# Six raw weight tiles instead of four and four split gated tiles instead of two, in a streaming-encoder layer on one Trainium2 core

## The chip, the core and the metric

The kernel runs on one core of a Trainium2 chip. A core has five engines that each work through their own list of instructions in order: TensorE (PE in the profile, with PEld for its weight loads) multiplies matrices, VectorE (DVE) and ScalarE (ACT) work on elements, GpSimd (POOL) does a little of it here, and SyncE (SP) issues nearly all the transfers, which sixteen DMA engines carry out. The metric is the device time of one execution in microseconds: the median of the runs, smaller is better.

## What is computed

One layer of a hybrid encoder on 256 tokens of width 4096, in float32. An input projection feeds 16 heads of forgetting attention (fox), 32 heads of an RWKV-7 recurrence, and a gate z; the gated outputs go through an output projection and a residual LayerNorm.

```python
proj = jnp.einsum('bsd,dc->bsc', x, w_in)
fox_cols, rw_cols, z = proj[..., :fox_end], proj[..., fox_end:fox_end + SHIFT_COLS], proj[..., fox_end + SHIFT_COLS:]
...
fox_out = _fox_attention(fq, fk, fv, log_f)
...
rw = rw + (rw_prev - rw) * mu_shift
...
y = _rwkv7_scan(rh, decay, kh, vh, -kk, kk * ah)
...
h = jnp.concatenate([fox_out, rwkv_out], axis=-1) * jax.nn.silu(z)
out = jnp.einsum('bsc,cd->bsd', h, w_out)
x = _layernorm(ALPHA * x + out, ln_gain, ln_bias, LN_EPS)
```

## The kernel before

**Precision.** Both projections are made of three matmuls for each product. A float32 tile is split into a high part (a cast to fp32r on ACT, suffix h) and a low part (the difference, on DVE, suffix l), and PE sums x_high times w_high, x_low times w_high, and x_high times w_low.

**Stages.** The first block, with the low-rank columns, runs from w_first. Then the loop at L1284 goes over eight groups n (two RWKV head pairs and two fox heads each), with four blocks b of 512 columns: b 0 holds r and k, b 1 the two kinds of v, b 2 and 3 fq, fk and the two halves of z for one fox head each. Behind the groups, the output projection (L1318) takes eight blocks of 512 columns, wo. In the trace a weight tile is w_q or wo_q, with q from 0 to 15: a tile is 128 rows by 1024 columns, two steps of 128 of the contraction, 512 KB, and feeds 12 matmuls of 512 columns.

**The weight stream.** load (L608) issues a weight's transfer into a raw tile of the tag wr, four buffers. fetch (L615) keeps up to three raw tiles waiting and splits the oldest (split, L521: four high buffers, three low ones). weights (L632) keeps three split tiles ready and hands the next to the matmuls. A raw buffer is free again once both its cast and its difference are done, and the next transfer into it waits for that on SyncE.

**Side work.** Between the matmuls of the blocks, slot (L592) advances generators: prepare turns r and k into the recurrence's operands, rwkv runs the recurrence of one group, fox the attention of one head, unload turns the projected columns by way of memory. In prepare the tile raw (r and k, turned) is loaded, ACT and DVE make the token shift s from it, then DVE forms k, sb and shl, and PE sums shl over head channels into np. In unload a fox head's fq is loaded (L1207), ACT scales it (L1211), and PE forms the scores fsp from it.

**The gate.** gate (L767) multiplies an output of either kind by its gate into h and splits h into hl. For a channel tile k below FAR (29), hl is stored to memory (hd, L780) and loaded back (h, get_h, L1217) while the last block runs, into the room of the x tiles that it no longer needs; the others stay on chip. The tag hl has two buffers, and the generator goes on only while fewer than two stores are under way.

**What sets the order.** All calls are only recorded (Later.take, L232). flush (L275) then makes an order for each engine from estimated durations, keeping a list of free buffers for each tag, and issues the instructions in it (L371), so every one of them has L372 in the profile. PE's main matmuls stand in their given order and side matmuls are placed between them. More buffers of a tag thus change the order that the planner writes as well as the waits on the chip.

**Room.** The program reserves, unless told otherwise, 16 KiB of each partition of the on-chip memory as a scratch for dynamic transfers that GpSimd issues. This kernel issues none from there: it issues its transfers from SyncE and, at the very start, two from ScalarE.

Of the kernel before, what the change touches and what calls it, by code (L numbers as in the profile page):

```python
# [12 lines left out]
F32 = mybir.dt.float32  # L13
# [6 lines left out]
P = 128  # L20
# [446 lines left out]
def layer(ctx: ExitStack, tc: tile.TileContext, xt, xtok, w_first, w_main, muv, w_o, up, par, mulora, fbias, lng, lnb, cst, out):  # L467
    nc = Later(tc)
# [4 lines left out]
    xpool = ctx.enter_context(tc.tile_pool(name="xpool", bufs=1))  # L473
    wpool = ctx.enter_context(tc.tile_pool(name="wpool", bufs=3))
# [19 lines left out]
    for n, (k0, k1) in enumerate(pieces):  # L494
        raw = spool.tile([P, 2 * S], F32, tag="xr", name=f"xr{n}", bufs=4)
        nc.sync.dma_start(out=raw[:, : (k1 - k0) * S], in_=xt[:, k0:k1, :].rearrange("p k t -> p (k t)"))
        x_raw.append(raw)
        raw = spool.tile([P, 4 * HALFB], F32, tag="fr", name=f"fr{n}", bufs=4)
# [22 lines left out]
    def split(src, n, name, pool=wpool, tag="", cols=1024):  # L521
        hi = pool.tile([P, cols], F32R, tag="wh" + tag, name=name + "h", bufs=4 if pool is wpool else 1)
        lo = pool.tile([P, cols], F32R, tag="wl" + tag, name=name + "l")
        nc.scalar.copy(hi[:, :n], src[:, :n])
        nc.vector.tensor_tensor(lo[:, :n], src[:, :n], hi[:, :n].bitcast(F32), ALU.subtract)
        return hi, lo
# [58 lines left out]
    def wait(n):  # L585
        for _ in range(n):
            yield
# [11 lines left out]
    stream = [(f"w{n}_{b}_{q}", w_main[n, b][:, 2 * q : 2 * q + 2, :]) for n in range(G // 2) for b in range(4) for q in range(KT // 2) if n or b]  # L599
# [6 lines left out]
    raws = []  # L606

    def load():  # L608
        if stream:
            name, src = stream.pop()  # L610
            raw = wpool.tile([P, 1024], F32, tag="wr", name=name, bufs=4)
            nc.sync.dma_start(out=raw, in_=src.rearrange("p k c -> p (k c)"))
            raws.append((name, raw))

    def fetch():  # L615
        while len(raws) < 3 and stream:
            load()
        if raws:
            name, raw = raws.pop(0)
            if name not in kept:  # L620
                ready.append((name, *split(raw, 1024, name)))
                return
            hl = []
            for j in range(4):
                hl.append(xpool.tile([P, OB], F32R, tag=f"x{4 * kept[name] + j}", name=f"{name}_{j}"))
            for j in range(2):
                r = raw[:, j * OB : (j + 1) * OB]
                nc.scalar.copy(hl[j], r)
                nc.vector.tensor_tensor(hl[2 + j], r, hl[j].bitcast(F32), ALU.subtract)
            ready.append((name, hl[:2], hl[2:]))  # L630

    def weights(name):  # L632
        nc.sooner = AHEAD
        while len(ready) < 3 and (stream or raws):
            fetch()
        nc.sooner = 0
        got, hi, lo = ready.pop(0)
        assert got == name
        return hi, lo
# [17 lines left out]
    rp = mid.enter_context(tc.tile_pool(name="rp", bufs=1))  # L657
# [18 lines left out]
    def issue(out, src):  # L676
        nc.sync.dma_start(out=out, in_=src)
# [77 lines left out]
    storing = []  # L755
# [10 lines left out]

    def gate(y, key, k):  # L767
        far = k < FAR
        while len(storing) > 1:
            yield  # L770
        h = rp.tile([P, S], F32, tag="h", name=f"h{k}")
        nc.vector.scalar_tensor_tensor(h, y, 0.5, szs[key], ALU.mult, ALU.mult)
        pool, tag, bufs = (rp, "hl", 2) if far else (xpool, f"x{k}", 1)
        hl = pool.tile([P, 2, S], F32R, tag=tag, name=f"hl{k}", bufs=bufs)
        nc.scalar.copy(hl[:, 0, :], h)
        nc.vector.tensor_tensor(hl[:, 1, :], h, hl[:, 0, :].bitcast(F32), ALU.subtract)
        if far:
            storing.append(k)
            yield from wait(SENT)
            issue(hd[k], flat(hl).bitcast(F32))  # L780
            kept_h.add(k)
            storing.remove(k)
        else:
            ht[k] = hl
# [6 lines left out]
    def flat(t):  # L791
        return t.rearrange("p a b -> p (a b)")
# [108 lines left out]
    def rwkv(n):  # L901
# [199 lines left out]
        for u in range(2):  # L1101
            nc.vector.reciprocal(sd[:, u], sd[:, u])
            yield
            nc.vector.tensor_tensor(yc[:, u], yc[:, u], sd[:, u], ALU.mult)
            nc.vector.tensor_tensor(yc[:, u], yc[:, u], bon[:, u], ALU.add)
            while f"r{i0 + u}" not in szs or 2 * (i0 + u) + 1 >= FAR and not closed:
                yield
            yield from gate(yc[:, u], f"r{i0 + u}", 2 * (i0 + u) + 1)
# [4 lines left out]
    def fox(i, q, k, vt):  # L1113
# [32 lines left out]
        while f"f{i}" not in szs or 2 * i >= FAR and not closed:  # L1146
            yield
        yield from gate(o, f"f{i}", 2 * i)
        foxed.add(i)

# [167 lines left out]
    for b, q in outs:  # L1318
        if q == 0:
            pool, tag = (ps, "ps") if b == 1 or b and b % 2 == 0 else (pp, "pp")  # L1320
# [3 lines left out]
        for j in range(2):  # L1324
            k = 2 * q + j
# [106 lines left out]
    for t, (i, h) in enumerate(order):  # L1432
# [10 lines left out]
        k, j, hi, lo = late[i]  # L1443
# [77 lines left out]
```

## Time and profile before

| | before |
|---|---|
| median of 3 runs, us | 1923.37 |
| lowest and highest, us | 1923.21, 1923.68 |
| the profiled execution, us | 1923.9 |
| its span from first to last instruction, us | 1922.1 |
| mean granted TensorE clock | 1.000 |
| share of the chain that ended last: PE | 95% |
| the same: DMA | 2% |
| read from and written to HBM, MB | 397.48, 38.26 |

The profile's page gives each engine's busy time. The windows view gives the same for chosen stretches. The waits view says which instruction waited for what and for how long. The chain view follows the work that ended last back in time, and the timeline shows single instructions with the idle time of their engine before them and what ended it in brackets. A row is read as start, duration, engine, line, operation, and what it writes and reads, with the tiles' shapes. An engine that idles costs nothing unless PE waits for it in the end.

### The profile page before, as it was taken

To read this page: it belongs to the slowest core of one execution; us is meant where nothing else is said; L and a number is where in the kernel's file an instruction comes from. 1 tells how busy PE (TensorE), PEld (TensorE's weight loads), DVE (VectorE), ACT (ScalarE), POOL (GpSimd) and SP (SyncE) were. 2 spreads that over 40 slices of the span, in tenths; PEclk is the share of its full clock that TensorE was granted. 3 is DMA by queue.
4 is the path that set the end of the run, shared out by engine and by line. 5 is a ranking of instruction groups with operands and counts; after the bars stand their busy time and mean duration, and the time that the engine had idled before them with its cause. 6 is when DMAs were issued, how large, how long until landed. Compare 5 with 4: busy or idle time off the path is not lost.

```text
span 1922.1 us, 28038 instructions
## 1 busy us (share of the span) xinstructions
PE 1909.9 (99%) x9965; PEld 1596.5 (83%) x9965; DVE 1408.4 (73%) x2290; ACT 970.1 (50%) x1434; POOL 42.4 (2%) x88
## 2 busy tenths in 40 slices
PE   9999999999999999999999999999999999999998
PEld 9888888888888888888888888888888788888887
DVE  6597778866886788669867885698678866755555
ACT  6464465455544554455446444554464444444332
POOL 0000000000000000000000000000000000000000
PEclk9999999999999999999999999999999999999999
DMA  9678877976698779867977797679777996866664
GB/s 353 186 219 252 232 199 207 266 220 199 206 272 230 198 204 262 220 199 210 274 223 207 201 265 216 199 214 269 220 213 197 357 277 195 294 201 202 189 195 164
DMA packets 340991, 437.60 MB, mean 228 GB/s; under 512 B 211682, under 2 KB 241988, under 8 KB 340852
## 3 DMA queue, kind: packets, MB, share of 16 engines
q1 hardware_dynamic: 340564, 435.45, 77.4%
q8 instruction: 78, 1.28, 0.3%
q14 instruction: 61, 0.50, 0.1%
q10 hardware_dynamic: 288, 0.37, 0.1%
HBM read 397.48 MB, written 38.26 MB: 227 GB/s over the span
## 4 chain that ended last, share of the span: by engine, by line
PE 95%; DMA 2%; DVE 2%; ACT 0%; issue 0%; ACTq 0%; SPq 0%; POOL 0%; DVEq 0%; POOLq 0%
PE acc L372 69%; PE oacc L372 17%; PE accl L372 2%; PE yp L372 1%; PE gp L372 1%; DMA w<-in_w_main_dram 1%; PE rh L372 1%; DMA wo<-in_w_o_dram 1%; PE up L372 1%; DMA hd<-hl 1%; PE lp L372 1%; PE fsp L372 1%; PE sp L372 1%; PE fop L372 0%; PE np L372 0%
## 5 line engine op out<-in xcount | busy, mean ns | idle before, releaser
L372 PE MATMUL acc<-w_9h,x 128*128 128x512 f32 x248 | 79.1, 398 | 0.0
L372 DVE TENSOR_TENSOR prod<-Nb,xc 128x8 f32<-128x8 f32 (+30 forms) x248 | 71.9, 290 | 9.7 <-DMA Nb<-nd 4.9
L372 PE MATMUL acc<-w_15h,x 128*128 128x512 f32 x248 | 78.8, 396 | 0.0
L372 PE MATMUL acc<-w_13h,x 128*128 128x512 f32 x248 | 78.8, 394 | 0.0
L372 PE MATMUL acc<-w_11h,x 128*128 128x512 f32 x248 | 78.6, 394 | 0.0
L372 PE MATMUL acc<-w_1h,x 128*128 128x512 f32 x248 | 78.3, 392 | 0.0
L372 PE MATMUL acc<-w_8h,x 128*128 128x512 f32 x248 | 78.0, 392 | 0.0
L372 PE MATMUL acc<-w_4h,x 128*128 128x512 f32 x248 | 78.0, 392 | 0.0
L372 PE MATMUL acc<-w_5h,x 128*128 128x512 f32 x248 | 77.7, 393 | 0.0
L372 PE MATMUL acc<-w_7h,x 128*128 128x512 f32 x248 | 77.7, 392 | 0.0
L372 PE MATMUL acc<-w_10h,x 128*128 128x512 f32 x248 | 77.6, 392 | 0.0
L372 PE MATMUL acc<-w_0h,x 128*128 128x512 f32 x248 | 77.5, 392 | 0.0
L372 PE MATMUL acc<-w_12h,x 128*128 128x512 f32 x248 | 77.1, 391 | 0.0
L372 PE MATMUL acc<-w_14h,x 128*128 128x512 f32 x248 | 77.0, 391 | 0.0
L372 PE MATMUL acc<-w_3h,x 128*128 128x512 f32 x248 | 76.9, 391 | 0.0
L372 PE MATMUL acc<-w_2h,x 128*128 128x512 f32 x248 | 76.8, 389 | 0.0
L372 PE MATMUL acc<-w_6h,x 128*128 128x512 f32 x248 | 76.4, 389 | 0.0
L372 DVE TENSOR_REDUCE xc<-prod 128x8 f32<-128x16 f32 (+30 forms) x248 | 72.3, 292 | 5.1
L372 ACT CAST w_11h<-w 128x1024 fp32r<-128x1024 f32 x31 | 32.7, 1054 | 56.1 <-PE acc L372 32.9
L372 ACT CAST w_15h<-w 128x1024 fp32r<-128x1024 f32 x31 | 32.6, 1052 | 51.2 <-PE acc L372 35.7
L372 DVE TENSOR_TENSOR w_0l<-w,w_0h 128x1024 fp32r<-128x1024 f32 x31 | 37.9, 1223 | 26.0 <-PE acc L372 23.4
L372 PEld LDWEIGHTS acc<-w_6h,x 128*128 128x128 f32 x248 | 46.6, 188 | 9.7
(625 smaller groups left out, 5477.8 us busy)
## 6 DMA issues: line engine op xcount, KB each, us to landing
w<-in_w_main_dram SPq DMA_DIRECT2D x496, 512.0 KB
wo<-in_w_o_dram SPq DMA_DIRECT2D x128, 512.0 KB
bt<-bk SPq DMA_DIRECT2D x96, 128.0 KB
fr<-in_w_first_dram SPq DMA_DIRECT2D x14, 720.0 KB
Nb<-nd SPq DMA_DIRECT2D x16, 512.0 KB
hd<-hl SPq DMA_DIRECT2D x29, 256.0 KB
h<-hd SPq DMA_DIRECT2D x29, 256.0 KB
raw<-bt SPq DMA_DIRECT2D x16, 256.0 KB
```

Of the source, the lines that this page charges most:

```text
L372: ins = op.call(*op.args, **op.kwargs)
```

## The change

The tag wr has six buffers instead of four, and fetch keeps up to five raw tiles waiting instead of three. The tag hl has four buffers instead of two, and a gate waits only while more than three stores are under way. Two raw tiles of 4 KiB and two hl tiles of 2 KiB in each partition, 12 KiB together, come out of the scratch, which shrinks from 16 KiB to 1 KiB.

```diff
--- before.py
+++ after.py
@@ -608,12 +608,12 @@
     def load():
         if stream:
             name, src = stream.pop()
-            raw = wpool.tile([P, 1024], F32, tag="wr", name=name, bufs=4)
+            raw = wpool.tile([P, 1024], F32, tag="wr", name=name, bufs=6)
             nc.sync.dma_start(out=raw, in_=src.rearrange("p k c -> p (k c)"))
             raws.append((name, raw))
 
     def fetch():
-        while len(raws) < 3 and stream:
+        while len(raws) < 5 and stream:
             load()
         if raws:
             name, raw = raws.pop(0)
@@ -766,11 +766,11 @@
 
     def gate(y, key, k):
         far = k < FAR
-        while len(storing) > 1:
+        while len(storing) > 3:
             yield
         h = rp.tile([P, S], F32, tag="h", name=f"h{k}")
         nc.vector.scalar_tensor_tensor(h, y, 0.5, szs[key], ALU.mult, ALU.mult)
-        pool, tag, bufs = (rp, "hl", 2) if far else (xpool, f"x{k}", 1)
+        pool, tag, bufs = (rp, "hl", 4) if far else (xpool, f"x{k}", 1)
         hl = pool.tile([P, 2, S], F32R, tag=tag, name=f"hl{k}", bufs=bufs)
         nc.scalar.copy(hl[:, 0, :], h)
         nc.vector.tensor_tensor(hl[:, 1, :], h, hl[:, 0, :].bitcast(F32), ALU.subtract)
@@ -1508,7 +1508,7 @@
     import concourse.bacc as _bacc
     from concourse.bass_utils import run_bass_kernel_spmd as _run
 
-    nc = _bacc.Bacc("TRN2", target_bir_lowering=False, num_devices=1)
+    nc = _bacc.Bacc("TRN2", target_bir_lowering=False, num_devices=1, dynamic_dma_scratch_size=1024)
     arrays, args = {}, []
     for name, a in arrange(inputs).items():
         arrays[f"in_{name}_dram"] = a
```

The same instructions are issued, and PE's list differs at three places only, in groups 3, 5 and 7, block 1. The lists of ACT and DVE differ in some dozens of rows by a place or two, and SyncE's by two weight tiles throughout. Three places follow. In all of them the numbers behind the last underscore only number the tiles.

**Group 3, block 1, ACT.** Here hl is the split of a gated output, s_6 the shifted r and k of channel tile 6. Before:

```order
L372 CAST hl_1773<-h_1772 128x256
L372 CAST w_1_10h<-w_1_10_1833 128x1024
L372 CAST w_1_11h<-w_1_11_1839 128x1024
L372 CAST hl_1820<-h_1819 128x256
L372 ACTIVATE s_6_1824<-raw_1813,omm 128x256
L372 ACTIVATE s_6_1825<-raw_1813,omm 128x256
L372 CAST w_1_12h<-w_1_12_1842 128x1024
```

With the change:

```order
L372 CAST hl_1775<-h_1774 128x256
L372 CAST w_1_10h<-w_1_10_1816 128x1024
L372 CAST hl_1822<-h_1821 128x256
L372 CAST w_1_11h<-w_1_11_1823 128x1024
L372 ACTIVATE s_6_1826<-raw_1815,omm 128x256
L372 ACTIVATE s_6_1827<-raw_1815,omm 128x256
L372 CAST w_1_12h<-w_1_12_1835 128x1024
```

The group's third hl cast (the second one shown) now stands ahead of the cast of weight tile 11, one place earlier.

**The same block, PE.** np is the sum of shl over head channels. Before:

```order
L372 MATMUL acc_1_0_1791<-w_1_11h,x_170 128x512 x2
L372 MATMUL acc_1_0_1791<-w_1_11l,x_170 128x512
L372 MATMUL acc_1_1_1792<-w_1_11h,x_170 128x512 x2
L372 MATMUL np_1848<-shl_1836,onesr 128x512 x2
L372 MATMUL acc_1_1_1792<-w_1_11l,x_170 128x512
```

With the change:

```order
L372 MATMUL acc_1_0_1793<-w_1_11h,x_170 128x512 x2
L372 MATMUL acc_1_0_1793<-w_1_11l,x_170 128x512
L372 MATMUL np_1850<-shl_1838,onesr 128x512 x2
L372 MATMUL acc_1_1_1794<-w_1_11h,x_170 128x512 x2
L372 MATMUL acc_1_1_1794<-w_1_11l,x_170 128x512
```

The pair of np moved ahead by two matmuls. In group 5 it moves by the same two, in group 7 by three.

**Group 7, block 3, SyncE.** w_3_q are the weights of block 3, h the gated tiles that come back, fq, fk and zf the turned columns of the fox head. Before:

```order
L372 DMA w_3_11_3302<-in_w_main_dram 128x1024
L372 DMA h_3328<-hd 128x512
L372 DMA w_3_12_3307<-in_w_main_dram 128x1024
L372 DMA h_3332<-hd 128x512
L372 DMA h_3333<-hd 128x512
L372 DMA fq_3282<-bt_2_3277 128x256
L372 DMA fk_3283<-bt_2_3277 128x256
L372 DMA zf_3284<-bt_2_3277 128x256
L372 DMA w_3_13_3315<-in_w_main_dram 128x1024
```

With the change:

```order
L372 DMA w_3_13_3304<-in_w_main_dram 128x1024
L372 DMA h_3330<-hd 128x512
L372 DMA w_3_14_3309<-in_w_main_dram 128x1024
L372 DMA h_3334<-hd 128x512
L372 DMA h_3335<-hd 128x512
L372 DMA fq_3284<-bt_2_3279 128x256
L372 DMA fk_3285<-bt_2_3279 128x256
L372 DMA zf_3286<-bt_2_3279 128x256
L372 DMA w_3_15_3317<-in_w_main_dram 128x1024
```

The three small loads stand behind the same h loads, but behind weight 14, and weight 15 follows them where weight 13 did.

**Output projection, third block, SyncE.** res, lg and lbias are loads for the residual and the LayerNorm. Before:

```order
L372 DMA wo_1_3503<-in_w_o_dram 128x1024
L372 DMA wo_2_15425<-in_w_o_dram 128x1024
L372 DMA res_15410<-in_xtok_dram 128x512
L372 DMA lg_15417<-in_lng_dram 128x512
L372 DMA res_15409<-in_xtok_dram 128x512
L372 DMA res_15410<-in_xtok_dram 128x512
L372 DMA lg_15444<-in_lng_dram 128x512
L372 DMA res_15409<-in_xtok_dram 128x512
L372 DMA res_15410<-in_xtok_dram 128x512
L372 DMA res_15409<-in_xtok_dram 128x512
L372 DMA wo_3_15428<-in_w_o_dram 128x1024
```

With the change:

```order
L372 DMA wo_3_3505<-in_w_o_dram 128x1024
L372 DMA wo_4_15429<-in_w_o_dram 128x1024
L372 DMA res_15414<-in_xtok_dram 128x512
L372 DMA lg_15421<-in_lng_dram 128x512
L372 DMA res_15413<-in_xtok_dram 128x512
L372 DMA res_15414<-in_xtok_dram 128x512
L372 DMA lg_15448<-in_lng_dram 128x512
L372 DMA res_15413<-in_xtok_dram 128x512
L372 DMA res_15414<-in_xtok_dram 128x512
L372 DMA res_15413<-in_xtok_dram 128x512
L372 DMA wo_5_15432<-in_w_o_dram 128x1024
```

The loads for the residual are the same; the weights ahead of, between and behind them are each two tiles further on.

## The prediction

> **What bounds the kernel now.** I read the page first: TensorE (PE) is busy for nearly the whole span.
>
> ```profile
> span 1922.1 us, 28038 instructions
> PE 1909.9 (99%) x9965; PEld 1596.5 (83%) x9965; DVE 1408.4 (73%) x2290; ACT 970.1 (50%) x1434; POOL 42.4 (2%) x88
> ```
>
> So the change can only pay where PE stands still: 1922.1 - 1909.9 = 12.2 us in all. The table of windows of 20 us says where. Its columns are the window, its length, PE busy with the number of matmuls, the granted clock, the DMA engines' share and GB/s.
>
> ```profile
> 660.00:680.00 20.00, 18.93 (x87) 1.00 0.75 237
> 1040.00:1060.00 20.00, 19.82 (x91) 1.00 0.79 251
> 1420.00:1440.00 20.00, 19.73 (x89) 1.00 0.80 258
> 1460.00:1480.00 20.00, 20.00 (x112) 1.00 0.66 182
> 1520.00:1540.00 20.00, 18.59 (x84) 1.00 1.04 408
> 1640.00:1660.00 20.00, 19.47 (x85) 1.00 0.99 357
> 1900.00:1920.00 20.00, 14.33 (x96) 1.00 0.48 197
> ```
>
> Between the first 20 us and 1900 only five windows fall short of 20.00, all shown (1460 to 1480 stands for the full ones), by 1.07, 0.18, 0.27, 1.41 and 0.53 us: 3.46 us. The rest of the 12.2 us is the start and the tail (the last row), which the change does not reach. The waits of PE name the five:
>
> ```profile
> PE np L372 <- DVE shl L372: 1.5, 3, 1.1
> PE fsp L372 <- ACT fq L372: 1.4, 1, 1.4
> PE oacc L372 <- DVE wo_5l L372: 0.5, 1, 0.5
> ```
>
> A stall is longer than its shortfall, because a matmul's record outlasts the time until the next one may start. The chain has 54 matmuls in 12.26 us, 0.227 us each; one record lasts 0.39 us. So each stall hides 0.39 - 0.227 = 0.16 us more.
>
> ```profile
> 677.78 12.26 PE acc L372 x54
> 672.84 0.39 PE L372 MATMUL acc<-w_11l,x 128*128 128x512 f32 x1
> 674.75 0.74 PE L372 MATMUL np<-shl,onesr 128*128 128x512 f32 x2 [1.07 <-DVE shl L372]
> ```
>
> The five stalls are therefore worth 3.46 + 5 x 0.16 = **4.3 us**. I call them A (1.23 us, group 3), B (0.34 and 0.43, groups 5 and 7), C (1.57, group 7, block 3) and D (0.69, output phase).
>
> **A and B: the third gated tile waits for a store.** ACT's, DVE's and SyncE's (SPq) rows of group 3, then what answers to them in groups 5 and 7:
>
> ```profile
> 658.71 0.38 SPq L372 DMA_DIRECT2D raw<-bt  x1
> 664.48 1.22 DVE L372 TENSOR_TENSOR w_10l<-w,w_10h 128x1024 fp32r<-128x1024 f32 x1 [0.60 <-PE acc L372]
> 667.74 0.41 ACT L372 CAST hl<-h 128x256 fp32r<-128x256 f32 x1 [2.44 <-DMA hd<-hl]
> 668.05 0.91 ACT L372 ACTIVATE s<-raw,omm 128x256 f32<-128x256 f32 x2
> 669.39 1.22 DVE L372 TENSOR_TENSOR w_11l<-w,w_11h 128x1024 fp32r<-128x1024 f32 x1
> 674.00 0.69 DVE L372 TENSOR_TENSOR shl<-sb,shl 128x512 fp32r<-128x512 f32 x1
> ...
> 1050.31 0.41 ACT L372 CAST hl<-h 128x256 fp32r<-128x256 f32 x1 [1.54 <-DMA hd<-hl]
> ...
> 1424.17 0.38 SPq L372 DMA_DIRECT2D raw<-bt  x1
> 1431.59 0.50 ACT L372 ACTIVATE s<-raw,omm 128x256 f32<-128x256 f32 x1
> 1433.21 0.41 ACT L372 CAST hl<-h 128x256 fp32r<-128x256 f32 x1 [1.12 <-DMA hd<-hl]
> ```
>
> ACT works in order. With two hl tiles, the third cast of a group waits for the first store to land (2.44, 1.54 and 1.12 us), and behind it wait s (the shifted r and k), then DVE's s, w_11l, k, sb and shl, and at last PE's np. With four tiles that wait goes. What is late next is raw or the pace of the weights. Raw: in group 7 s ran 1431.59 - 1424.17 = 7.4 us after raw's issue, so in group 3 raw is in by 658.71 + 7.4 = 666.1, which lets s start 1.9 us sooner. Weights: a tile feeds 12 matmuls, 2.72 us; w_11l may follow w_10l by that, at 667.2 instead of 669.39, 2.2 us sooner. The smaller is 1.9 us. Needed are the stall and the new place of np: PE now has it two matmuls (0.45 us) earlier in groups 3 and 5 and three (0.68) in group 7. Group 3: 1.23 + 0.45 = 1.68 against 1.9. Group 5: 0.34 + 0.45 = 0.79 against 1.54. Group 7: 0.43 + 0.68 = 1.11 against 1.12. All three go, group 7 barely by these rows; up to 0.3 us may stay there. **Gain 2.0 us** (1.7 to 2.0). The gate's own wait (more than one store under way) gives way to three, which only lets the same 29 stores be issued earlier.
>
> **C: fq stands behind a late weight.** The stretch around it, the issue of fq and of the weight behind it, and ACT:
>
> ```profile
> 1500.00:1532.00 32.00, 30.70 (x136) 24.98 (x134) 25.80 (x53) 14.99 (x19) 0.00 (x0) 1.00 1.06 375
> ...
> 1522.55 0.32 SPq L372 DMA_DIRECT2D fq<-bt  x1
> ...
> 1525.09 5.51 DMA w<-in_w_main_dram
> ...
> 1530.69 1.04 ACT L372 CAST w_13h<-w 128x1024 fp32r<-128x1024 f32 x1 [2.58 <-DMA w<-in_w_main_dram]
> 1531.64 0.41 ACT L372 ACTIVATE fq<-fq 128x256 f32<-128x256 f32 x1
> ```
>
> Here the DMA engines are full (share 1.06), since the h tiles come back from memory beside the weights. w_13 was issued at 1525.09, took 5.51 us, and ACT held fq's scaling behind its cast. With six raw tiles w_13 is issued ahead of fq, not behind it, and is two tiles (2 x 2.72 = 5.4 us of PE) further ahead of its use; what is late next is fq itself. By the same 5.5 us it lands at 1528.1 and is scaled by 1528.5, 2.0 us ahead of the 1530.5 at which PE wants it (it was ready at 1532.05, which is 1.57 us late). **Gain 1.6 us** (0 if fq comes later by more than 3.6, see the first rival).
>
> **D: weights behind a burst of 256 KB loads.** Two issues on the chain, and what ACT and DVE did with them:
>
> ```profile
> 1639.90 7.89 DMA wo<-in_w_o_dram
> 1651.31 5.74 DMA wo<-in_w_o_dram
> ...
> 1652.46 1.05 ACT L372 CAST wo_4h<-wo 128x1024 fp32r<-128x1024 f32 x1 [3.51 <-DMA wo<-in_w_o_dram]
> 1657.15 1.05 ACT L372 CAST wo_5h<-wo 128x1024 fp32r<-128x1024 f32 x1 [2.60 <-DMA wo<-in_w_o_dram]
> 1658.23 1.23 DVE L372 TENSOR_TENSOR wo_5l<-wo,wo_5h 128x1024 fp32r<-128x1024 f32 x1 [1.82 <-ACT wo_5h L372]
> ```
>
> Now wo_5 takes the place in SyncE's order that wo_3 had (issued 1639.90, landed 1647.8) and wo_7 that of wo_5 (landed 1657.05). wo_7's low part can then be ready at 1659.5, and PE wants it two tiles, 5.4 us, after it wanted wo_5's (ready at 1659.46, 0.69 late: 1658.8): 1664.2. So the stall goes with 4.7 us to spare. **Gain 0.7 us** (0 to 0.7).
>
> **What is costed at nothing.** No byte, cast or matmul is added. A weight's issue still waits for the DVE split that frees its buffer; six deep, it waits for a split six tiles back where it was four, and its place in the queue is two tiles earlier, so at an even pace each issue falls at the time it had and carries a tile from two further on. That hides it; if it fails, each small transfer behind comes later by up to two tiles, which is the third rival. Other moves on ACT and DVE are by one or two instructions. The scratch: the trace has no software queue that could use it.
>
> ```profile
> q1 hardware_dynamic: 340564, 435.45, 77.4%
> q8 instruction: 78, 1.28, 0.3%
> q14 instruction: 61, 0.50, 0.1%
> q10 hardware_dynamic: 288, 0.37, 0.1%
> ```
>
> The same rows say that all traffic shares SyncE's queue. [...]
>
> **Sum.** 2.0 + 1.6 + 0.7 = 4.3 us. The profiled execution took 1923.9 us (1922.1 of span and 1.8 around it), and would take 1919.6. The median of the runs is 1923.37, 0.5 less, so I predict 1923.4 - 4.3 = **1919.1 us**. The restart after each stall is slower by perhaps 0.1 us (np's pair took 0.74 against 0.62 to be expected of 0.227 + 0.39), which could add 0.5: 1918.6.
>
> **Rivals.**
> 1. *fq behind two more tiles.* fq stands behind the same 14 h loads but 15 weights instead of 13. If the two extra tiles have not landed before the full stretch, 1.05 MB at 408 GB/s put fq 2.6 us later, 1530.7, scaled at 1531.1: 0.6 us of C stays, 1919.7; with 0.3 left in each of A and B too, 1920.6. For it: the share of 1.06. Against: the lead is gained before the stretch, where the share is 0.66. Chance 0.24.
> 2. *The change does not reach C and D.* If bandwidth alone makes the weights late there (share 1.04 and 0.99), a lead is used up before the stall and both stay: only 2.0 us go, 1921.4. Against: the lead is 5.4 us of PE, more than either stall. Chance 0.13.
> 3. *Slower: raw behind the weights.* If the two tiles stand ahead of raw as well, raw lands 2.6 us later in each group, and np, now earlier in PE's order, waits in odd groups 2.6 less about 0.3 of margin: 3 x 2.3 = 6.9 us. Groups 1, 2, 4 and 6, which have no stall now, lose 0 to 2.3 each, 4.6 at the middle. 1919.1 + 6.9 + 4.6 = 1930.6 (from 1926.0). It decides once raw lands more than 0.3 us later than now. Against: the share around group 3 is 0.75, not full, and the issues keep their times. Chance 0.06.
>
> **How the numbers follow.** Forecast 0.57, rivals 0.24, 0.13, 0.06. A measurement of this kernel can tell about 0.2%, 3.85 us, so faster means under 1919.5. The forecast's spread of 1918.6 to 1919.8 lies mostly, not all, below that: 0.47 faster. The first two rivals and the rest of the forecast are 0.47 within 0.2%. Slower 0.06. The range takes in the forecast and the first two rivals with half a microsecond on either side: 1918.1 to 1921.9.
>
> **What would show it.** Right: the five windows read 20.00 and PE's waits list neither np, fsp nor oacc; ACT's hl has no wait for hd; w_13h and wo_5h have none for a weight; PE's idle time is about 8.7 us. Wrong at A and B: np still waits for shl, with s now behind raw. Wrong at C: fq's scaling waits for its own transfer. Wrong altogether: a new wait of PE in groups 1, 2, 4 or 6, or raw landing later after its issue than 7.4 us.

## The result and the profile after

The change takes 1919.74 us (median of 22 runs, 1918.56 to 1920.64) against 1923.20 us for the kernel before, run beside it (22 runs, 1921.14 to 1924.97): a ratio of 0.9982, 95% interval 0.9975 to 0.9989. The profiled execution took 1919.61 us, 1917.8 of them span. TensorE's busy time and the span on the page of the change:

```profile
span 1917.8 us, 28038 instructions
PE 1909.0 (100%) x9965; PEld 1597.6 (83%) x9965; DVE 1410.9 (74%) x2290; ACT 971.1 (51%) x1434; POOL 43.5 (2%) x88
```

PE idles 8.8 us instead of 12.2. The windows of 20 us that were short before (columns: window, length, PE busy with its matmuls, granted clock, share of the DMA engines, GB/s), with the last row for the tail:

```profile
660.00:680.00 20.00, 20.00 (x92) 1.00 0.80 263
1040.00:1060.00 20.00, 20.00 (x94) 1.00 0.82 261
1420.00:1440.00 20.00, 20.00 (x91) 1.00 0.80 264
1520.00:1540.00 20.00, 20.00 (x91) 1.00 1.04 409
1640.00:1660.00 20.00, 20.00 (x90) 1.00 0.99 352
1900.00:1920.00 20.00, 10.00 (x61) 0.88 0.52 210
```

All five are full, and PE's list of waits is down to three, none of them of the old places:

```profile
PE zp L372 <- DVE zd L372: 1.3, 1, 1.3
PE warmup L372 <- POOL idle L372: 1.0, 1, 1.0
PE wp L372 <- ACT l L372: 0.2, 1, 0.2
```

**Group 3 (A).** The timeline of the change: the third hl cast waits only for its input, s follows 1.3 us later, and shl is ready at 671.75 + 0.68 = 672.43, 1.16 us before np runs.

```profile
664.44 0.41 ACT L372 CAST hl<-h 128x256 fp32r<-128x256 f32 x1 [1.33 <-DVE h L372]
665.73 0.90 ACT L372 ACTIVATE s<-raw,omm 128x256 f32<-128x256 f32 x2
671.75 0.68 DVE L372 TENSOR_TENSOR shl<-sb,shl 128x512 fp32r<-128x512 f32 x1
673.59 0.63 PE L372 MATMUL np<-shl,onesr 128*128 128x512 f32 x2
```

**Group 7, block 3 (C).** fq is issued at 1519.54 (before: 1522.55). w_13's cast waits for PE's use of the tiles, not for its transfer, and fq is scaled by 1526.68, 2.06 us before fsp:

```profile
1519.54 0.32 SPq L372 DMA_DIRECT2D fq<-bt  x1
1525.31 1.06 ACT L372 CAST w_13h<-w 128x1024 fp32r<-128x1024 f32 x1 [1.66 <-PE acc L372]
1526.27 0.41 ACT L372 ACTIVATE fq<-fq 128x256 f32<-128x256 f32 x1
1528.74 0.82 PE L372 MATMUL fsp<-fk,fq 128*128 128x128 f32 x4
```

**Output phase (D).** Weights still come late behind the 256 KB loads (wo_7's cast waits 2.76 us for its transfer), but the low part is ready at 1657.31, 3.0 us before PE uses the tile:

```profile
1653.88 1.05 ACT L372 CAST wo_7h<-wo 128x1024 fp32r<-128x1024 f32 x1 [2.76 <-DMA wo<-in_w_o_dram]
1656.09 1.22 DVE L372 TENSOR_TENSOR wo_7l<-wo,wo_7h 128x1024 fp32r<-128x1024 f32 x1
1660.32 0.62 PE L372 MATMUL oacc<-wo_7h,h 128*128 128x512 f32 x2
```

The two profiled spans differ by 1922.1 - 1917.8 = 4.3 us, the medians by 3.5. The experiments had to show which part brings what, and why these two numbers differ.

### The profile page after: what moved, and what is told of

It is laid out like the page before. It is cut to its first block, busy times and chain, and to the rows that moved or that the text cites. A ratio compares the mean times of both kernels' runs of the same rounds, so it can differ in the third digit from the quotient of the medians.

```text
span 1917.8 us, 28038 instructions
## 1 busy us (share of the span) xinstructions
PE 1909.0 (100%) x9965; PEld 1597.6 (83%) x9965; DVE 1410.9 (74%) x2290; ACT 971.1 (51%) x1434; POOL 43.5 (2%) x88
## 3 DMA queue, kind: packets, MB, share of 16 engines
q8 instruction: 78, 1.28, 0.3%
## 4 chain that ended last, share of the span: by engine, by line
PE 99%; DVE 0%; ACT 0%; issue 0%; ACTq 0%; POOL 0%; POOLq 0%
PE acc L372 73%; PE oacc L372 18%; PE accl L372 2%; PE yp L372 1%; PE gp L372 1%; PE rh L372 1%; PE up L372 1%; PE lp L372 1%; PE sp L372 1%; PE fop L372 1%; PE fsp L372 1%; PE np L372 0%; PE xp L372 0%; PE qt L372 0%; PE vs L372 0%; PE warmup L372 0%
```

## The experiments

Three sets, each run beside the kernel before on one chip. "Short" is the sum by which PE's busy time falls short in the windows of 20 us between 20 and 1900, in the one profiled execution.

| run | what differs from the kernel before | median, us | before, us | ratio, 95% interval | span, us | short, us |
|---|---|---|---|---|---|---|
| e0_change | the change again | 1919.71 | 1923.23 | 0.9982 (0.9973 to 0.9991) | 1918.8 | 1.05 |
| e1_raw6_only | six raw tiles, five ahead | 1920.93 | 1923.23 | 0.9988 (0.9979 to 0.9997) | 1919.3 | 0.99 |
| e2_hl4_only | four hl tiles | 1921.75 | 1923.23 | 0.9992 (0.9983 to 1.0001) | 1919.9 | 1.41 |
| e3_scratch_only | the small scratch | 1922.68 | 1923.23 | 0.9999 (0.9990 to 1.0008) | 1919.5 | 1.38 |
| e4_raw6_look3 | six raw tiles, three ahead | 1921.13 | 1922.84 | 0.9992 (0.9983 to 1.0001) | 1918.7 | 0.80 |
| e5_hl3 | three hl tiles | 1921.19 | 1922.84 | 0.9992 (0.9983 to 1.0001) | 1923.8 | 3.30 |
| e6_raw5 | five raw tiles, four ahead | 1922.70 | 1922.84 | 1.0001 (0.9992 to 1.0010) | 1920.7 | 2.49 |
| e7_fq_pool | fq scaled on GpSimd | 1924.09 | 1922.84 | 1.0006 (0.9997 to 1.0014) | 1921.8 | 3.38 |
| e9_raw5_again | as e6 | 1922.55 | 1922.76 | 1.0002 (0.9993 to 1.0010) | 1919.7 | 1.59 |
| e10_raw6_hl3 | six raw tiles, three hl tiles | 1918.92 | 1922.76 | 0.9982 (0.9973 to 0.9991) | 1917.6 | 0.00 |
| e11_before_again | nothing | 1922.94 | 1922.76 | 1.0002 (0.9994 to 1.0011) | 1920.9 | 1.94 |
| e12_change_again | the change again | 1919.64 | 1922.76 | 0.9985 (0.9977 to 0.9994) | 1919.9 | 1.87 |

e11, the kernel before against itself, says how fine the comparison is: about 0.1% either way. All kernels but e11 have the scratch of 1 KiB.

### The parts one at a time

e3 is the last hunk of the diff alone. e1 adds the raw tiles, e2 the hl tiles:

```diff
 e1
-            raw = wpool.tile([P, 1024], F32, tag="wr", name=name, bufs=4)
+            raw = wpool.tile([P, 1024], F32, tag="wr", name=name, bufs=6)
-        while len(raws) < 3 and stream:
+        while len(raws) < 5 and stream:
 e2
-        while len(storing) > 1:
+        while len(storing) > 3:
-        pool, tag, bufs = (rp, "hl", 2) if far else (xpool, f"x{k}", 1)
+        pool, tag, bufs = (rp, "hl", 4) if far else (xpool, f"x{k}", 1)
```

> Six raw tiles, but two hl tiles and the old gate. My theory: C and D go, A and B stay, since ACT's third hl cast still waits for a store: 2.3 us less than before (ratio 0.9988), np waits for shl three times, 1.5 us by the page. Rival (the weights' lead is what frees A and B too, since w_11 comes earlier): all five go, 4.3 us less, 0.9978. Rival (bandwidth, not the lead, makes C and D): nothing goes, 1.000.

> Four hl tiles and the wider gate, but four raw tiles. My theory: A and B go, C and D stay: 2.0 us less (ratio 0.9990); PE waits for fsp 1.4 us and for oacc 0.5 us as before. Rival (np, now two or three matmuls earlier in PE's order, needs the weights' lead as well): np still waits for shl in one or more groups, and the gain is under 1 us.

> Only the scratch is cut from 16 KiB to 1 KiB; every engine's order is that of the kernel before, and all tiles lie 15 KiB lower. My theory: no difference, 1.000 within 0.001, and the five stalls as before. Rival (the scratch or the tiles' addresses matter to the transfers): a difference of 1 us or more, or stalls of another size.

PE's waits in e1, the first fence, and in e2, the second (waited for: us in total, times, longest). The waits named zp, warmup and wp are in every kernel and are not shown:

```profile
PE np L372 <- DVE shl L372: 1.0, 2, 0.8
```

```profile
PE oacc L372 <- DVE wo_5l L372: 0.5, 1, 0.5
PE oacc L372 <- ACT wo_5h L372: 0.5, 1, 0.5
PE fsp L372 <- ACT fq L372: 0.4, 1, 0.4
```

The raw tiles take away C and D and leave A and B; the hl tiles take away A and B and leave C and D. The medians go the same way: 2.3 us less with the one (0.9988), 1.5 with the other (0.9992, whose interval just reaches 1), and 3.5 with both; the parts add up within their intervals. The scratch alone (e3) is worth nothing that can be measured, and its order of instructions is that of before.

For C the list of waits is not enough, since e3 has no fsp wait either. What separates the kernels is how long before fsp the scaling of fq ends. With four raw tiles w_13's cast waited 2.5 to 2.6 us for its transfer in all five profiles with fq on ScalarE, and fq was ready 0.35 us (e3) or 0.05 us (e11, below) early, or fsp waited 0.39 (e2), 1.41 (before) or 2.23 us (e5). With five or six raw tiles w_13's cast waits for PE's use of the tiles in all eight profiles, and fq was ready 1.9 to 2.1 us early in seven of them; the eighth, e12, is taken up below. For D the list is enough: all six profiles with four raw tiles have an oacc wait for wo_5, and none of the eight with more has one.

### Are all the tiles needed?

e4 keeps six raw tiles but looks only three ahead; e5 has three hl tiles; e6 five raw tiles, four ahead; e10 is the change with three hl tiles:

```diff
 e4, against the change
-        while len(raws) < 5 and stream:
+        while len(raws) < 3 and stream:
 (and gate and hl as in the kernel before)
 e5 and e10
-        while len(storing) > 1:
+        while len(storing) > 2:
-        pool, tag, bufs = (rp, "hl", 2) if far else (xpool, f"x{k}", 1)
+        pool, tag, bufs = (rp, "hl", 3) if far else (xpool, f"x{k}", 1)
 e6
-            raw = wpool.tile([P, 1024], F32, tag="wr", name=name, bufs=4)
+            raw = wpool.tile([P, 1024], F32, tag="wr", name=name, bufs=5)
-        while len(raws) < 3 and stream:
+        while len(raws) < 4 and stream:
```

> Six raw tiles, but still only three loads ahead of the cast; two tiles of split outputs, scratch 1024. Theory 1 (the gain at C and D comes from the tile that a load no longer has to wait for, so that SyncE is not held at it, and the request stands ahead of the bursts): fsp and oacc waits gone as with five ahead, np waits stay (1 to 1.5 us together), time 1920.9 as the run with six raw tiles and look-ahead 5. Rival (the gain comes from the number of loads ahead, 2.5 MB against 1.5 MB under way): fsp and oacc waits stay in the profile, time 1922.7 to 1923.2.

> Three tiles of split gated outputs in place of four, gate open for up to two stores under way; four raw tiles, scratch 1024. Theory (only the third cast of a group met a tile that was still being stored, so one tile more is enough): no np wait, fsp and oacc waits of 0 to 1.6 us each as they fall, time 1921.7 as the run with four. Rival (the store is so late that the fourth tile counts too): np waits stay at 0.3 to 1 us, time 1922.5 to 1923.2.

> The change with three tiles of split outputs in place of four (gate open for up to two stores), six raw tiles as in the change. Theory (the fourth tile has no part in the gain): no np, fsp or oacc wait, time as that of the change, 1919.7, ratio to it within 0.1%. Rival (the fourth tile counts once the weights run further ahead): np waits of 0.3 us or more, time 1920.3 to 1921.

e4 has no fsp and no oacc wait, and an np wait of 0.7 us is left. So it is the room, not the number of loads counted as ahead, that takes C and D away. e5 has no np wait: three hl tiles do what four do, since a group meets the ring only at its third cast. e10 confirms it with the weights: PE waits for nothing but zp, warmup and wp, as in the profile of the change, and its 1918.92 cannot be told from the 1919.64 of the change beside it. The fourth hl tile has no part in the gain that these runs can show.

> Five raw tiles, four loads ahead; two tiles of split outputs, scratch 1024. Theory (the weights were late at C and D by under 2.7 us, which is less than the time between two weight casts, so one tile more covers it): fsp and oacc waits gone, np waits stay, time 1921.0. Rival (each of the two tiles counts): fsp or oacc wait of 0.3 us or more stays, time 1921.8 to 1922.3.

> The kernel with five raw tiles once more, since its first time (1922.7, no gain) does not go with its profile (no fsp wait, no oacc wait). Theory 1 (chance: the np waits came out large, 0.9, 0.8 and 0.8 us, in that measurement): fsp and oacc waits gone again, np waits 0.7 to 1.5 us together, time 1.5 to 2.3 us under that of the kernel before. Rival (five tiles bring a lasting loss of their own: the stores of the split outputs land later, so that each of the three np waits is about 0.8 us): np waits again 2 us or more together, time within 0.8 us of that of the kernel before.

Here the expectation failed. Both profiles with five raw tiles have neither an fsp nor an oacc wait, and yet the medians (1922.70, 1922.55) are only 0.1 and 0.2 us under that of before. What grew is B, in group 7 of both and in group 5 of e6 (0.82 us, elsewhere at most 0.36). A, 0.89 and 0.80 us, lies among the other profiles with two hl tiles (0.67 to 1.07). PE's np waits, e6 and then e9:

```profile
PE np L372 <- DVE shl L372: 2.5, 3, 0.9
```

```profile
PE np L372 <- DVE shl L372: 1.5, 2, 0.8
```

In group 7 of both, from the issue of the first hd store to the third hl cast that waits for it, 7.0 us passed; in the six other profiles with two hl tiles 6.4 to 6.6. The rows of e6, which give 1434.61 - 1427.59 = 7.02, and the wait that they end in, 0.78 us (0.74 in e9) against 0.13 to 0.33 in those six:

```profile
1427.59 0.39 SPq L372 DMA_DIRECT2D hd<-hl  x1
1434.61 0.41 ACT L372 CAST hl<-h 128x256 fp32r<-128x256 f32 x1 [1.50 <-DMA hd<-hl]
1441.33 0.71 PE L372 MATMUL np<-shl,onesr 128*128 128x512 f32 x2 [0.78 <-DVE shl L372]
```

So in these two profiles the store landed later, and part of what C and D give was lost at B. Why it lands later is not shown: e1 and e4, with six raw tiles, are among the six. B covers some 0.5 us of e9, whose profiled execution was the fastest of its eleven (1921.54), not the whole of the missing 2 us. A further 0.2 us lies outside the span: a run of e6 or e9 takes 1.9 to 2.0 us more than its span (the median of the eleven), one of before 1.8. But e1 and e4 have that too (2.0 to 2.1), so it does not set five tiles apart from six. Why five are worth so much less stays open.

### Is C the cast in ScalarE's queue?

e7 leaves all room as before and only takes fq's scaling out from behind the casts:

```diff
-        nc.scalar.mul(fq, fq, FOX_SCALE)
+        nc.gpsimd.tensor_scalar(fq, fq, FOX_SCALE, None, ALU.mult)
```

> Rooms as before (four raw tiles, two split outputs, scratch 1024); the scaling of fq runs on GpSimd in place of ScalarE, so it stands behind no weight cast. Theory (C is ScalarE's in-order queue: a cast whose weights are late holds the scaling that a matmul waits for): no fsp wait in the profile though the casts of group 7, block 3 still wait for their weights, np and oacc waits stay, time 1921.9 to 1923 (0 to 1.4 us less than before, as C falls in an execution). Rival (TensorE stops there because fq itself lands late, or it stops at the late weights instead): a wait of fsp for GpSimd or of acc for a w_13 or w_14 tile of 0.4 us or more appears, time 1923.2 or more.

fq landed at 1528.88 and GpSimd scaled it at once, ready at 1530.57; w_13h's cast ended only at 1531.91, and ScalarE's next instruction ran from 1531.81. By an estimate from that start and the 0.41 us that the scaling took in the kernel before, it would have been ready on ScalarE at 1532.2, 1.6 us later. There is no fsp wait any more. But the weights stayed late (w_11h's cast waits 2.13 us for its transfer; the wait of w_13h's is put down to xc on VectorE, so there the profile does not name the transfer), and the next thing on which PE waits behind a late cast is the eviction bk, ScalarE's copy of a finished sum. GpSimd, ScalarE and PE in the timeline of e7:

```profile
1525.31 1.05 ACT L372 CAST w_11h<-w 128x1024 fp32r<-128x1024 f32 x1 [2.13 <-DMA w<-in_w_main_dram]
1528.88 1.69 POOL L372 TENSOR_SCALAR fq<-fq 128x256 f32<-128x256 f32 x1 [57.70 <-DMA fq<-bt]
1530.86 1.05 ACT L372 CAST w_13h<-w 128x1024 fp32r<-128x1024 f32 x1 [2.60 <-DVE xc L372]
1545.59 0.58 ACT L372 COPY bk<-acc 128x512 f32<-128x512 f32 x1
1546.22 0.74 PE L372 MATMUL oacc<-wo_0h,h 128*128 128x512 f32 x2 [1.28 <-ACT bk L372]
```

And the chain of e7 shows what held that eviction, the transfer of a weight, then its cast wo_2h on ScalarE:

```profile
1537.75 6.79 DMA wo<-in_w_o_dram
1544.64 0.04 ACT wo_2h L372
1545.59 0.59 ACT bk L372
```

fq no longer stands behind the late cast, as the theory has it, but nothing is saved: PE stood still for 1.28 us 16 us later, and the median, 1924.09, is above the 1921.9 to 1923 expected and not lower than before. That moving fq brought this stall is not shown: the kernel before has it too in e11 below, at 0.67 us. (PE's fsp moved by a place or two in its list as well, so e7 is not a clean trade of one instruction.) No profile with five or six raw tiles has a bk stall, which speaks for curing the late weight and not the victim.

### How much of it belongs to one execution?

e11, e0 and e12 are the kernels before and after, unchanged.

> The kernel before, run as if it were a change: a second profile of it, and the measure of what the timing tells apart. Theory (the stalls A to D are the same places in every execution, but their lengths are not: the profiled execution behind the forecast had 4.3 us of them, the usual one some 3.5): ratio 1.000 with its interval on both sides; np waits in groups 3, 5 and 7, and one or both of fsp and oacc, 2.5 to 4 us together. Rival (the lengths belong to the kernel, and the forecast missed something else): the same 4.3 us, each within 0.2 us of its first length.

> The changed kernel once more, for a second profile of it. My theory: PE waits for neither np, fsp nor oacc again, and the time is 3.4 us under the kernel before (ratio 0.9982). If the first profile was a lucky one, one of the five stalls (0.3 to 1.6 us) is back, which would explain why the medians differ by 3.5 us and the profiled executions by 4.3.

> The change once more, beside the other three: a third profile of it. Theory (the stop of fop at pT is a place that only some executions of the change reach, and costs about 1 us where they do): none of the five old waits, the fop wait there or not there, 0 to 1.2 us; time 1919.2 to 1920.2, and the span of the profiled execution longer by about the fop wait where it shows. Rival (a stall of the old list can come back in the change as well): an np, fsp or oacc wait of 0.3 us or more.

The second profile of before has A at 0.7 us and D at 0.4, no B in the list and no C. Instead the late weight wo_2 holds the eviction bk there, the stall that e7 showed. Its waits of PE, and two rows of ScalarE:

```profile
PE np L372 <- DVE shl L372: 0.7, 1, 0.7
PE oacc L372 <- ACT bk L372: 0.7, 1, 0.7
PE oacc L372 <- DVE wo_5l L372: 0.4, 1, 0.4
```

```profile
1543.79 1.05 ACT L372 CAST wo_2h<-wo 128x1024 fp32r<-128x1024 f32 x1 [2.14 <-DMA wo<-in_w_o_dram]
1544.74 0.58 ACT L372 COPY bk<-acc 128x512 f32<-128x512 f32 x1
```

Its short windows sum to 1.94 us where the first profile of before has 3.46. e3, in the same order, has A, B in group 7 and D at 0.74, 0.28 and 0.36 us. So the places recur, but not every one in every execution, and their lengths change. A shows what sets its length: the np wait of group 3 is the time from the hd store's issue to the cast that waits for it, less 5.96 us, in the two profiles of before (667.74 - 660.71 = 7.03 with 1.07; 667.83 - 661.14 = 6.69 with 0.73) and in e1, e4 and e7 (6.78 with 0.82, 6.63 with 0.67, 6.91 with 0.95). In these five profiles, the later the store landed, the longer PE waited, microsecond for microsecond.

The change has a stall of its own in two of its three profiles: fop, the product of a fox head's turned scores pT with its values, waits for pT. First e0, then e12:

```profile
1548.91 2.79 SPq L372 DMA_DIRECT2D pT<-fpt  x1
1555.69 0.89 PE L372 MATMUL fop<-pT,vt 128*128 128x256 f32 x4 [1.05 <-DMA pT<-fpt]
```

```profile
1522.58 0.32 SPq L372 DMA_DIRECT2D fq<-bt  x1
1525.25 1.06 ACT L372 CAST w_13h<-w 128x1024 fp32r<-128x1024 f32 x1 [1.67 <-PE acc L372]
1528.68 0.42 ACT L372 ACTIVATE fq<-fq 128x256 f32<-128x256 f32 x1 [2.37 <-DMA fq<-bt]
1529.15 0.92 PE L372 MATMUL fsp<-fk,fq 128*128 128x128 f32 x4 [0.31 <-ACT fq L372]
1556.81 0.89 PE L372 MATMUL fop<-pT,vt 128*128 128x256 f32 x4 [1.56 <-DMA pT<-fpt]
```

In the first profile of before there were 1558.07 - 1551.10 = 7.0 us from pT's issue to fop, which waited for nothing. In e0 PE was at fop 3.4 us sooner (1555.69 - 1.05 = 1554.64), by the stalls that are gone, but the issue came only 2.2 us sooner. That left 5.7 us for a transfer that took 6.6 (the chain has 6.64 for it). The first profile of the change had 1554.72 - 1548.62 = 6.1 us, and there the transfer came in within them. In e12 the issue came as late as in before (1551.09), and the same holds for fq: it was issued at 1522.58 against 1522.55 and landed 6.1 us later, while PE wanted it 1.9 us sooner (1528.84 against 1532.11 - 1.41 = 1530.70). The weights are in time there, as w_13h's wait for PE shows, and fq's own transfer is what is late: 0.31 us. Why SyncE issued both 2.5 to 3.0 us later in e12 than in the first profile of the change is not shown.

## Why the prediction came out as it did

**A and B: right in mechanism, and larger in margin.** The store no longer holds the third cast (e2, e5), and all three np waits go. Group 3 had 1.16 us to spare after the change, where the prediction counted 1.9 - 1.68 = 0.22. Group 7 had 0.79 (1437.57 - 1436.78), where it counted 0.01, and the 0.3 us that might stay there did not.

**C: right for two of three executions, and its margin by luck.** In the profile beside the timing fq was scaled 2.06 us before fsp, where the prediction had 2.0. But the prediction had fq's landing as what comes last, at 1528.1, against PE at 1530.5. That is a time of before; with A and B gone, PE is there 1.8 to 1.9 us sooner. And the scaling stood behind w_13's cast, which PE's own pace held (1.66 us), so that seven of the eight profiles with more raw tiles have 1.9 to 2.1 us, though fq was issued anywhere from 8.4 to 10.2 us ahead of fsp in them. In e12 that issue was as late as in before, and fq itself took 0.31 us of C's place, as in the first rival. The rival's reason is not what the runs show: it had fq held up 2.6 us by two weights more ahead of it, 5.5 + 2.6 = 8.1 us from issue to landing, and fq took 6.1 us in e12 (1522.58 to 1528.68). The 2.6 us was the author's estimate, two tiles at 408 GB/s, and no run shows it. The measured median is the 1919.7 of this rival by chance only.

**D: right.** Weights still come late there and PE does not wait for them. The margin is 3.0 us, not 4.7, since the working again took PE's time of before: 1664.2, where PE uses wo_7 from 1660.32.

**The second and third rival did not happen.** No np wait for a late raw tile appears in any group of the change's three profiles (in group 3 of the first, s ran 665.73 - 659.24 = 6.5 us after raw's issue, where the third rival had 7.4 + 2.6), and C and D are reached by the raw tiles alone (e1, e4).

**The sum: right for its own execution, and 0.6 us too low for the median.** The profiled execution was to take 1923.9 - 4.3 = 1919.6, and the one of the change took 1919.61 (PE idles 8.8 us, forecast 8.7); the 0.5 us that quicker restarts might have added did not show. The step that failed is the next one, "The median of the runs is 1923.37, 0.5 less, so I predict 1923.4 - 4.3 = 1919.1": it took stalls that one execution had away from a median whose executions have fewer of them. The profiled execution of before lies 0.7 us above the median of the 22 runs (1923.9 against 1923.20), that of the change 0.1 us below its own (1919.61 against 1919.74); this is the 0.8 us between the spans' 4.3 and the medians' 3.5. The second profile of before has 1.94 us of short windows and four stalls, 1.94 + 4 x 0.16 = 2.6 us, by the prediction's own rule. And a term was left out: what PE, sooner at its later places, finds late there. fop's wait, 1.05 us in e0 and 1.56 in e12, is that term. Both executions took longer than the median of their eleven (1920.58 against 1919.71, 1921.68 against 1919.64), so how much of it the median holds is not shown.

## What to carry to other kernels

On an engine that works in order, cure what arrives late and not the instruction that happens to stand behind it: with fq moved away from the late cast PE waited 1.28 us for the next victim instead (bk in e7), while room for two more of the late tiles left no such stall in any profile. Read stalls of a microsecond from more than one execution before you subtract them from a median, and when stalls in sequence go, recompute the time at which the engine wants each later tile, since everything behind them is wanted sooner by their sum (fop by 3.4 us in e0). Add buffers up to the wait that is seen and measure each step: the third hl tile did all that the fourth did (1918.92 us in e10 against 1919.64 in e12), and the fifth raw tile alone brought nothing that could be measured (0.1 and 0.2 us in e6 and e9).

## What the runs showed of the hardware that was not expected

One long stall was followed by a loss beyond its own length. In e5's profiled execution, the slowest of its eleven (1925.61 us against a median of 1921.19), C was 2.23 us long, and TensorE's granted clock fell to a half behind it. The windows of 2 us of e5 (columns as above):

```profile
1528.00:1530.00 2.00, 1.57 (x7) 1.00 1.01 378
1530.00:1532.00 2.00, 0.20 (x1) 1.00 0.99 377
1532.00:1534.00 2.00, 2.00 (x9) 0.82 0.99 327
1534.00:1536.00 2.00, 2.00 (x6) 0.50 1.04 396
1536.00:1538.00 2.00, 2.00 (x8) 0.82 1.01 394
```

From its timeline, the stall between two pairs of matmuls of one kind, 0.62 us before it and 1.05 at the halved clock:

```profile
1528.05 0.62 PE L372 MATMUL acc<-w_10h,x 128*128 128x512 f32 x2
1531.80 0.92 PE L372 MATMUL fsp<-fk,fq 128*128 128x128 f32 x4 [2.23 <-ACT fq L372]
1534.50 1.05 PE L372 MATMUL acc<-w_11h,x 128*128 128x512 f32 x2
```

The clock missing from the three rows, by estimate 2 x (0.18 + 0.50 + 0.18) = 1.7 us, comes on top of the 2.23. Stalls of 1.4 us (C before) and 1.56 us (fop in e12) left the clock at 1.00 in their windows of 20 us. The fall is from one execution; that the stall brought it, or how long a stall has to be for it, is not shown. The change also takes away the slowest runs: the slowest of its 44 took 1921.68 us, the slowest of the 88 of the kernel before beside them 1925.34. Whether a halved clock made those slow is not shown.
